# A hybrid attention and gating block in fp32: the order from the first norm to the sixth product written out on four engines

## The chip, the cores and the metric

The kernel runs on one core of a Trainium2 chip. Its work is shared by TensorE (PE, matrix products and transposes), VectorE (DVE), ScalarE (ACT), GpSimd (POOL) and the queues that issue DMA transfers, the main one on SyncE (SP). The metric is the device time of one execution in microseconds.

## The reference

One residual block over 1024 positions of width 1024: a norm, one wide projection `w_in`, a gated linear attention and a spatial gating unit, their merge, and a SwiGLU feed-forward layer, all in fp32.

```python
a = rmsnorm(x, norm_pre_mix[l])
proj = jnp.einsum('bsd,de->bse', a, w_in[l])
q, k, v, r, a_low, su, sv, g_gla, g_sgu = jnp.split(proj, IN_OFFSETS, axis=-1)
y_gla = gla_branch(q, k, v, r, a_low, w_gate_up[l], b_gate[l], gla_norm[l])
y_sgu = sgu_branch(su, sv, sgu_ln_g[l], sgu_ln_b[l], w_spatial[l], b_spatial[l])
merged = (jax.nn.sigmoid(g_gla) * jnp.einsum('bsv,vd->bsd', y_gla, w_branch_gla[l])
          + jax.nn.sigmoid(g_sgu) * jnp.einsum('bsv,vd->bsd', y_sgu, w_branch_sgu[l]))
x = x + rmsnorm(jnp.einsum('bsd,de->bse', merged, w_out[l]), norm_post_mix[l])
h = rmsnorm(x, norm_pre_ffn[l])
gate, up = jnp.split(jnp.einsum('bsd,df->bsf', h, w_ffn_in[l]), 2, axis=-1)
y = jnp.einsum('bsf,fd->bsd', jax.nn.silu(gate) * up, w_ffn_out[l])
x = x + rmsnorm(y, norm_post_ffn[l])
```

## The kernel before

An fp32 product is made of three products of rounded parts: each operand is split into hi (ScalarE's copy to the type fp32r, L86) and lo (VectorE's difference, L87), and `prod3` multiplies hi by hi, hi by lo and lo by hi (L110, L111, L112). The large products are blocked in two by two and need seven products of blocks instead of eight. In place of the eighth product stand sums and differences of blocks of both operands (`wsum` or, in place, `raw` for the weights), numbered m1 to m7; a product of one such number is 12 matmuls of 128x512.

A `Pair` is two blocks of 128 output columns, fetched as two raw weight tiles. `prepare(m)` makes the weight sum if m needs one (m5 and m7 at L257, m6 at L262, m4 at L265) and splits it; `product(m)` issues the 12 matmuls and then `collect`, which adds the results up on VectorE and ScalarE. m1 reads the first half of the columns of x tiles 4 to 7 and m2 the second half, m5 reads the sum of both halves of tiles 0 to 3. A `Stream` runs the pairs; its first three (the trio: su0, su1 and kq0 here) are taken together: m1 of su0 and su1, m2 of both, m1 and m2 of kq0, then m5 of the three, m7, m6, m4 and m3. There are two streams, over `w_in` from the start and over `w_ffn_in` from about 920 us.

At the start, the gain row is spread over 128 partitions by two matmuls (gb). Then for each of the tiles 4, 5, 6, 7, 0, 1, 2, 3 `norm_tile` squares the tile on ScalarE with the sum along the row, forms the factor on VectorE (L105) and GpSimd (a pow, L101), scales 1024 columns on VectorE (L406), and `A.tile` turns them by eight TensorE transposes into two PSUM banks (L170) and copies these to the raw tiles in SBUF on ScalarE (L172). From the raw tiles `first` splits for m1 and m2 (tiles 4 to 7), `second` adds the halves and splits for m5 (tiles 0 to 3), both at L86 and L87.

PSUM has eight banks, four of them for accumulators (`bank`), four for transposes and the like (`tbank`). The order on each engine is set by the scheduler of the tile framework, apart from SP's, which is written out; an engine works off its list in that order, and an instruction that waits holds up all behind it.

Of the kernel before, what the change touches and what calls it, by code (L numbers as in the profile page):

```python
# [10 lines left out]
AF = mybir.ActivationFunctionType  # L11
ALU = mybir.AluOpType
# [3 lines left out]
P = 128  # L16
D = 1024
# [14 lines left out]
def hybrid_block(ctx, tc, I, out):  # L32
    nc = tc.nc
# [34 lines left out]
    def slot(name, shape=(P, 1024), dt=F32):  # L68
        return px.tile(list(shape), dt, tag="X", name=name)
# [12 lines left out]
    def small(name, shape):  # L82
        return pm.tile(shape, F32, tag="m", name=name)
# [5 lines left out]
    def by4(t):  # L89
        return t.rearrange("p (a b) -> p a b", a=4)  # L90
# [6 lines left out]
    ident = cst.tile([P, P], F32, name="ident")  # L97
# [45 lines left out]
    class Operands:  # L143
# [11 lines left out]
                self.raw[r, c] = big(F32, f"{self.name}raw{r}{c}")  # L155
            return self.raw[r, c]

        def put(self, m, src, cols):
            if m not in self.hl:
                self.hl[m] = (big(F32R, f"{self.name}h{m}"), big(F32R, f"{self.name}l{m}"))  # L160
            hi, lo = self.hl[m]
            return split(hi[:, :, cols], lo[:, :, cols], src)

        def tile(self, row, tt, gains=None):
            r = 1 - tt // 4
            cols = slice((tt % 4) * P, (tt % 4) * P + P)
            for c in range(2):
                b = tbank(f"tp_{self.name}{tt}{c}")
                for j in range(4):
                    nc.tensor.transpose(b[:, j * P : (j + 1) * P], row[:, (c * 4 + j) * P : (c * 4 + j + 1) * P], ident)  # L170
                if gains is None:
                    nc.scalar.activation(self.quad(r, c)[:, :, cols], by4(b), AF.Copy)  # L172
                    continue
                for j in range(4):
                    nc.scalar.activation(self.quad(r, c)[:, j, cols], b[:, j * P : (j + 1) * P], AF.Copy,
                                         scale=gains[:, c * 4 + j : c * 4 + j + 1])

        def first(self, tt):
            cols = slice((tt % 4) * P, (tt % 4) * P + P)
# [40 lines left out]
    ORDER = (1, 7, 6, 5, 2, 4, 3)  # L220

    behind = {}

    class Pair:

# [24 lines left out]
        def prepare(self, m):  # L250

            a, b = self.raw
            w11, w12, w21, w22 = a[:, :, 0:P], a[:, :, P:256], b[:, :, 0:P], b[:, :, P:256]
            tt = nc.vector.tensor_tensor
            if m in (5, 7):
                src = w12 if self.trio and m == 7 else py.tile([P, 4, P], F32, tag="Y", name=f"wsum_{self.name}{m}")
                tt(out=src, in0=(w12, w22)[m == 7], in1=(w11, w12)[m == 7], op=ALU.subtract)  # L257
                if m == 7:
                    self.chain = src
            elif m == 6:  # L260
                src = self.chain
# [10 lines left out]
        def product(self, m, A):  # L272
            hi, lo = A.hl[m]
            w = self.w.pop(m)
            base = {2: 1, 4: 7, 3: None if self.p5 else 5}.get(m)
            new = tbank if self.trio and m == 6 else bank
            acc = self.acc[m] = self.acc[base] if base else new(f"{self.name}_m{m}")
            for k in range(4):
                prod3(acc, w[:, 0, k], w[:, 1, k], hi[:, k], lo[:, k], base is None and k == 0, k == 3, base is not None)
            self.collect(m, acc)  # L280

        def collect(self, m, acc):

# [44 lines left out]
    LEAD = 2  # L328

    class Stream:  # L330
# [69 lines left out]
    def norm_tile(tt):  # L400
        xt = xts[tt]
        a = slot(f"a_{tt}")
        ss = small(f"ss_{tt}", [P, 1])
        nc.scalar.activation(a, xt, AF.Square, accum_out=ss)
        rs = rsqrt_mean(ss, D, f"a{tt}")
        nc.vector.scalar_tensor_tensor(out=a, in0=xt, scalar=rs, in1=g_pre, op0=ALU.mult, op1=ALU.mult)  # L406
        A.tile(a, tt)
# [404 lines left out]
    one_row = slot("one_row", (1, P))  # L812
    nc.vector.memset(one_row, 1.0)
    g_pre = slot("g_pre")
    for j in range(2):
        b = tbank(f"gb_{j}")
        nc.tensor.matmul(b, lhsT=one_row, rhs=g_row[:, j * 512 : j * 512 + 512], start=True, stop=True)
        nc.vector.tensor_copy(g_pre[:, j * 512 : j * 512 + 512], b)
    for tt in (4, 5, 6, 7):
        norm_tile(tt)  # L820
        A.first(tt)
    stream.prepare(4)
    for tt in (0, 1, 2, 3):
# [247 lines left out]
    for half, j, fin in ((1, 0, False), (1, 1, True), (0, 1, False), (0, 0, True)):  # L1071
        w = wo10 if (half, j) == (1, 0) else out_weights(half, j)
        for tt in range(half * 4, half * 4 + 4):
            acc = (tbank if (half, j) == (1, 0) else bank)(f"wo_{tt}{j}")
            c = slice((tt % 4) * P, (tt % 4) * P + P)
            for kt in range(KT):
                hi, lo = mT[kt // 4][half]
# [7 lines left out]
            mix, ss = mixes[tt]  # L1085
            scaled_half(mix, ss, acc, j, g_pm)
            if fin:
                if tt in (2, 3):
                    xt = slot(f"xr_{tt}")
                    nc.sync.dma_start(out=xt, in_=x[tt * P : (tt + 1) * P, :])  # L1090
                else:
                    xt = load(f"xr_{tt}", x[tt * P : (tt + 1) * P, :])
                rs = both(ss, f"pm{tt}")
# [3 lines left out]
                rs = rsqrt_mean(ss[:, 3:4], D, f"pf{tt}")  # L1097
# [102 lines left out]
```

## Time and profile before

| | us |
|---|---|
| median of 3 runs | 1552.12 (1550.65 to 1552.93) |
| the profiled execution | 1552.86 |
| its span | 1550.9 |
| PE busy in it | 1523.6 (98%) |
| DVE, ACT, POOL busy | 1130.2, 661.6, 177.8 |

The span is the part of an execution that the profile covers. Busy time is the union of an engine's instructions, so that PE's idle time is the span less 1523.6 us. For matmuls the profile models the ends: a matmul starts each 0.23 us at full clock, and its row shows 0.39 us.

### The profile page before, as it was taken

To read this page: it belongs to the slowest core of one execution; us is meant where nothing else is said; L and a number is where in the kernel's file an instruction comes from. 1 tells how busy PE (TensorE), PEld (TensorE's weight loads), DVE (VectorE), ACT (ScalarE), POOL (GpSimd) and SP (SyncE) were. 2 spreads that over 40 slices of the span, in tenths; PEclk is the share of its full clock that TensorE was granted. 3 is DMA by queue.
4 is the path that set the end of the run, shared out by engine and by line. 5 is a ranking of instruction groups with operands and counts; after the bars stand their busy time and mean duration, and the time that the engine had idled before them with its cause. 6 is when DMAs were issued, how large, how long until landed. Compare 5 with 4: busy or idle time off the path is not lost.

```text
span 1550.9 us, 19786 instructions
## 1 busy us (share of the span) xinstructions
PE 1523.6 (98%) x7061; PEld 1243.9 (80%) x7061; DVE 1130.2 (73%) x1853; ACT 661.6 (43%) x1100; POOL 177.8 (11%) x275
## 2 busy tenths in 40 slices
PE   6999999899999999999999999999999999999998
PEld 5778777677888888888888887888888888888886
DVE  7966676577888878648796769877777876564547
ACT  7566333344444343444333675333333333363442
POOL 2112111011211111000000110111111110000002
PEclk9999999999999999999999999999999999999999
DMA  5134453245664364488972631656555643875653
GB/s 192 32 123 124 148 177 123 69 152 181 216 218 157 129 213 139 162 313 300 346 275 90 208 119 55 221 194 202 188 176 161 200 158 102 302 267 174 226 157 129
DMA packets 181844, 276.06 MB, mean 178 GB/s; under 512 B 10801, under 2 KB 108625, under 8 KB 181746
## 3 DMA queue, kind: packets, MB, share of 16 engines
q1 hardware_dynamic: 157714, 190.35, 38.5%
q0 software_dynamic: 24032, 84.45, 14.8%
q8 instruction: 56, 0.92, 0.2%
q14 instruction: 42, 0.34, 0.1%
HBM read 188.48 MB, written 86.28 MB: 177 GB/s over the span
## 4 chain that ended last, share of the span: by engine, by line
PE 94%; DVE 3%; ACT 1%; issue 1%; DMA 0%; POOL 0%; SPq 0%; DVEq 0%; POOLq 0%; ACTq 0%
PE f_m L110 8%; PE f_m L112 8%; PE f_m L111 8%; PE fo L110 5%; PE fo L111 5%; PE fo L112 5%; PE g_m L110 3%; PE g_m L112 3%; PE g_m L111 3%; PE wo L110 2%; PE wo L111 2%; PE wo L112 2%; PE kq_m L110 2%; PE su_m L111 2%; PE kq_m L112 2%; PE su_m L112 2%
## 5 line engine op out<-in xcount | busy, mean ns | idle before, releaser
L110 PE MATMUL f_m<-hh,w_f 128*128 128x512 f32 x616 | 239.7, 390 | 1.8 <-ACT w_f L86 1.1
L111 PE MATMUL f_m<-hl,w_f 128*128 128x512 f32 x616 | 239.8, 389 | 0.0
L112 PE MATMUL f_m<-hh,w_f 128*128 128x512 f32 x616 | 239.5, 389 | 0.0
L110 PEld LDWEIGHTS f_m<-hh,w_f 128*128 128x128 f32 x616 | 115.6, 188 | 26.3 <-issue 1.5
L112 PEld LDWEIGHTS f_m<-hh,w_f 128*128 128x128 f32 x616 | 115.6, 188 | 24.2 <-DVE w_f L87 0.2
L111 PEld LDWEIGHTS f_m<-hl,w_f 128*128 128x128 f32 x616 | 115.6, 188 | 24.1
L111 PE MATMUL fo<-fow,foa 128*128 128x512 f32 (+1 forms) x315 | 120.9, 384 | 0.0
L112 PE MATMUL fo<-fow,foa 128*128 128x512 f32 (+1 forms) x315 | 120.9, 384 | 0.0
L110 PE MATMUL fo<-fow,foa 128*128 128x512 f32 (+1 forms) x315 | 118.9, 385 | 0.5 <-DVE foc L935 0.5
L86 ACT ACTIVATE w_f<-raw_f 128x512 fp32r<-128x512 f32 x75 | 47.2, 633 | 104.7 <-PE f_m L112 88.5
L86 ACT ACTIVATE w_f<-wsum_f 128x512 fp32r<-128x512 f32 x79 | 49.9, 633 | 95.2 <-PE f_m L112 52.8
L87 DVE TENSOR_TENSOR w_f<-wsum_f,w_f 128x512 fp32r<-128x512 f32 x79 | 54.3, 688 | 48.1 <-ACT w_f L86 47.6
L111 PE MATMUL g_m<-al,w_g 128*128 128x512 f32 x224 | 88.3, 394 | 0.0
L110 PE MATMUL g_m<-ah,w_g 128*128 128x512 f32 x224 | 88.2, 394 | 0.0
L112 PE MATMUL g_m<-ah,w_g 128*128 128x512 f32 x224 | 87.8, 392 | 0.0
L87 DVE TENSOR_TENSOR foa<-fora,foa 128x1024 fp32r<-128x1024 f32 (+1 forms) x42 | 47.6, 1133 | 43.1 <-ACT foa L86 43.0
L86 ACT ACTIVATE foa<-fora 128x1024 fp32r<-128x1024 f32 (+1 forms) x42 | 41.5, 988 | 73.7 <-DMA fora<-fs_d 62.3
L110 PEld LDWEIGHTS fo<-fow,foa 128*128 128x128 f32 x315 | 59.2, 188 | 12.6 <-DVE foc L935 0.7
L112 PEld LDWEIGHTS fo<-fow,foa 128*128 128x128 f32 x315 | 59.2, 188 | 11.8
L111 PEld LDWEIGHTS fo<-fow,foa 128*128 128x128 f32 x315 | 59.2, 188 | 11.6
L87 DVE TENSOR_TENSOR fow<-forw,fow 128x1024 fp32r<-128x1024 f32 (+1 forms) x42 | 47.4, 1129 | 9.9 <-ACT fow L86 9.8
L87 DVE TENSOR_TENSOR w_f<-raw_f,w_f 128x512 fp32r<-128x512 f32 x75 | 51.2, 685 | 4.1 <-ACT w_f L86 3.9
(396 smaller groups left out, 3698.0 us busy)
## 6 DMA issues: line engine op xcount, KB each, us to landing
raw_f<-in_w_ffn_in SPq DMA_DIRECT2D x88, 256.0 KB, 3.4
fora<-fs_d SPq DMA_DIRECT2D x35, 512.0 KB, 4.4
fs_d<-f_o POOLq DMA_DIRECT2D x22, 512.0 KB, 3.8
w2e<-in_w_ffn_out SPq DMA_DIRECT2D x44, 256.0 KB, 4.5
ws_d<-w2e POOLq DMA_DIRECT2D x22, 512.0 KB, 3.7
forw<-ws_d SPq DMA_DIRECT2D x20, 512.0 KB, 4.7
raw_g<-in_w_in SPq DMA_DIRECT2D x16, 512.0 KB, 3.8
g_d<-g_o POOLq DMA_DIRECT2D x16, 512.0 KB, 4.8
```

Source lines behind the costliest of these rows:

```text
L86: a = nc.scalar.activation(hi, src, AF.Copy)
L87: return a, nc.vector.tensor_tensor(out=lo, in0=src, in1=hi, op=ALU.subtract)
L110: nc.tensor.matmul(acc, lhsT=lh, rhs=rh, start=first, stop=False, skip_group_check=onto)
L111: nc.tensor.matmul(acc, lhsT=lh, rhs=rl, start=False, stop=False, skip_group_check=onto)
L112: nc.tensor.matmul(acc, lhsT=ll, rhs=rh, start=False, stop=last, skip_group_check=onto)
```

## The change

`norm_tile` is gone. Its steps are now small functions, and the order of PE, ACT, DVE and POOL from the gain row through the sixth product is written out. hi of tiles 4 to 7 is copied straight from the transposes' PSUM bank (`high`), lo is the difference of the bank and hi (`low_part`), and the raw copies (`keep`) come later. The scale of tiles 4 to 7 is done in halves, and the bank for a tile's second half is an accumulator's for some. `fifth` adds the halves of tiles 0 to 3 from the bank of one and the raw copy of the other. `collect` of the first six products is put into the list `later_on` and called where the order says. The weights of the low-rank gate (`wa`) are fetched on GpSimd's queue before the pows. The weight sums of both trios are made by GpSimd (in the second stream all but m5's, by `early`).

```diff
-            tt = nc.vector.tensor_tensor
+            tt = (nc.gpsimd if self.trio and (m != 5 or early) else nc.vector).tensor_tensor
...
-            self.collect(m, acc)
+            if later_on is not None:
+                later_on.append(lambda: self.collect(m, acc))
+            else:
+                self.collect(m, acc)
...
-    for tt in (4, 5, 6, 7):
-        norm_tile(tt)
-        A.first(tt)
-    stream.prepare(4)
-    for tt in (0, 1, 2, 3):
-        norm_tile(tt)
-        A.second(tt)
+    def high(tt, c):
+        cols = slice((tt - 4) * P, (tt - 4) * P + P)
+        nc.scalar.activation(A.parts(1 + c)[0][:, :, cols], by4(turned[tt, c]), AF.Copy)
+
+    def low_part(tt, c):
+        cols = slice((tt - 4) * P, (tt - 4) * P + P)
+        hi, lo = A.parts(1 + c)
+        nc.vector.tensor_tensor(out=lo[:, :, cols], in0=by4(turned[tt, c]), in1=hi[:, :, cols], op=ALU.subtract)
+
+    def keep(tt, c):
+        A.keep(tt, c, turned[tt, c])
+
+    def fifth(tt):
+        cols = slice(tt * P, tt * P + P)
+        s1 = A.quad(2, 0)[:, :, cols]
+        nc.vector.tensor_tensor(out=s1, in0=by4(turned[tt, 1]), in1=A.raw[1, 0][:, :, cols], op=ALU.add)
+        A.put(5, s1, cols)
...
     low_rank_weights()
-    stream.fetch(3)
-    stream.run(6)
-    low_rank_sums()
+    with tc.manual_schedule(engines={ET.PE, ET.Activation, ET.DVE, ET.Pool}):
...
+        stream.prepare(1)
+        high(6, 0), low_part(6, 0), high(7, 0), low_part(7, 0)
+        go()
+        stream.prepare(2)
+        scale(6, 1), turn(6, 1, bank)
+        keep(4, 0)
+        high(4, 1), high(5, 1)
+        scale(7, 1), turn(7, 1, tbank)
+        low_part(4, 1), low_part(5, 1)
+        keep(4, 1)
+        high(6, 1), low_part(6, 1)
+        square(0)
+        high(7, 1), low_part(7, 1)
+        go()
...
+        for tt in (0, 1):
+            for c in range(2):
+                turn(tt, c, tbank)
+        scale(2, 0, 1)
+        keep(0, 0), keep(1, 0)
+        square(3), factor(3)
+        go()
+        stream.prepare(6)
+        fifth(0), fifth(1)
+        keep(0, 1), keep(1, 1)
+        scale(3, 0, 1)
+        for tt in (2, 3):
+            for c in range(2):
+                turn(tt, c, tbank)
+        keep(2, 0), keep(3, 0)
+        later_on[4]()
+        go()
+        fifth(2), fifth(3)
+        keep(2, 1), keep(3, 1)
+        keep(6, 1)
+        stream.prepare(7)
+        low_rank_sums()
+        for i in (2, 3, 5):
+            later_on[i]()
+    later_on = None
     stream.run(3)
...
+    early = False
```

`go` runs one product with the next weights not yet prepared; `turn` issues the four transposes of a half tile. The order moves on each engine as follows. First VectorE before, from the factor of tile 2 on: `a` is a scaled tile, `araw` a raw one or the sum of two, `al` lo of the activations, `w_kq` lo of the weights of kq.

```order
35 L105 TENSOR_SCALAR rs_a_322<-ss_320 128x1
36 L186 TENSOR_TENSOR araw_291<-araw_282,araw_289 128x4x128
37 L105 TENSOR_SCALAR rs_a_344<-ss_342 128x1
38 L406 SCALAR_TENSOR_TENSOR a_319<-xx_147,rs_a_322,g_pre 128x1024
39 L186 TENSOR_TENSOR araw_291<-araw_282,araw_289 128x4x128
40 L406 SCALAR_TENSOR_TENSOR a_341<-xx_147,rs_a_344,g_pre 128x1024
41 L87 TENSOR_TENSOR al_294<-araw_291,ah_293 128x4x128
42 L87 TENSOR_TENSOR w_kq_402<-raw_kq_366,w_kq_402 128x512
43 L87 TENSOR_TENSOR al_294<-araw_291,ah_293 128x4x128
```

The same place in the changed kernel, from the fifth product's weights on.

```order
36 L87 TENSOR_TENSOR w_kq_355<-raw_kq_349,w_kq_355 128x512
37 L837 SCALAR_TENSOR_TENSOR a_330<-xx_147,rs_a_334,g_pre 128x1024
38 L105 TENSOR_SCALAR rs_a_388<-ss_386 128x1
39 L87 TENSOR_TENSOR w_kq_404<-raw_kq_352,w_kq_404 128x512
40 L860 TENSOR_TENSOR araw_407<-tp_a_366,araw_382 128x4x128
41 L87 TENSOR_TENSOR al_410<-araw_407,ah_409 128x4x128
42 L860 TENSOR_TENSOR araw_407<-tp_a_376,araw_382 128x4x128
43 L87 TENSOR_TENSOR al_410<-araw_407,ah_409 128x4x128
44 L837 SCALAR_TENSOR_TENSOR a_385<-xx_147,rs_a_388,g_pre 128x1024
```

Before, the scales of tiles 2 and 3 (rows 38 and 40) stand two rows apart, and one sum of halves lies between them; now both `fifth` steps of tiles 0 and 1 (rows 40 to 43) stand between the scale of tile 2 (row 37) and that of tile 3 (row 44).

Then ScalarE before, after the first copy of a transposes' bank: L172 are the raw copies, L86 with `ah` hi of the activations.

```order
7 L86 ACTIVATE w_su_258<-raw_su_136 128x512
8 L172 ACTIVATE araw_179<-tp_a_174 128x4x128
9 L86 ACTIVATE ah_181<-araw_172 128x4x128
10 L172 ACTIVATE araw_172<-tp_a_196 128x4x128
11 L86 ACTIVATE ah_185<-araw_179 128x4x128
12 L172 ACTIVATE araw_179<-tp_a_202 128x4x128
13 L86 ACTIVATE ah_181<-araw_172 128x4x128
14 L404 ACTIVATE a_270,ss_271<-xx_140 128x1024
```

ScalarE in the changed kernel, from the first weight split on: L847 is hi from the bank, L187 a raw copy, L829 the square, `w_su_251` the weights of the second pair.

```order
8 L86 ACTIVATE w_su_231<-raw_su_136 128x512
9 L847 ACTIVATE ah_213<-tp_a_218 128x4x128
10 L847 ACTIVATE ah_213<-tp_a_225 128x4x128
11 L86 ACTIVATE w_su_251<-raw_su_143 128x512
12 L187 ACTIVATE araw_260<-tp_a_175 128x4x128
13 L847 ACTIVATE ah_262<-tp_a_187 128x4x128
14 L847 ACTIVATE ah_262<-tp_a_205 128x4x128
15 L187 ACTIVATE araw_274<-tp_a_187 128x4x128
16 L847 ACTIVATE ah_262<-tp_a_255 128x4x128
17 L829 ACTIVATE a_278,ss_279<-xx_140 128x1024
```

The raw copies have gone behind the first splits, and the weight split of the second pair (row 11) stands ahead of the first of them and of all splits for m2.

Last GpSimd in the changed kernel, from the last of the eight pows on; before, the memset of `aw` followed the pows there.

```order
24 L101 TENSOR_TENSOR rs_a_388<-rs_a_388,mhalf 128x1
25 L270 TENSOR_TENSOR wsum_su_465<-raw_su_136 128x512
26 L270 TENSOR_TENSOR wsum_su_510<-raw_su_143 128x512
27 L270 TENSOR_TENSOR raw_su_136<-raw_su_138,raw_su_136 128x4x128
28 L270 TENSOR_TENSOR raw_su_143<-raw_su_145,raw_su_143 128x4x128
29 L270 TENSOR_TENSOR wsum_kq_515<-raw_kq_349 128x512
30 L270 TENSOR_TENSOR raw_kq_349<-raw_kq_352,raw_kq_349 128x4x128
31 L275 TENSOR_TENSOR raw_su_136<-raw_su_136 128x4x128
32 L275 TENSOR_TENSOR raw_su_143<-raw_su_143 128x4x128
```

The weight sums (L270) follow the last pow (row 24) in the order m5 and m7 of su0 and su1, then those of kq0.

## Rows read from the trace of the kernel before

**Rows 1.** The page: busy time by engine, and the chain that ended last

```profile
PE 1523.6 (98%) x7061; PEld 1243.9 (80%) x7061; DVE 1130.2 (73%) x1853; ACT 661.6 (43%) x1100; POOL 177.8 (11%) x275
...
PE 94%; DVE 3%; ACT 1%; issue 1%; DMA 0%; POOL 0%; SPq 0%; DVEq 0%; POOLq 0%; ACTq 0%
```

**Rows 2.** Waits of PE: engine, line, releaser: us in total, times, longest

```profile
PE tp_a L170 <- ACT w_su L86: 4.9, 1, 4.9
PE tp_a L170 <- DVE a L406: 3.9, 2, 2.9
...
PE o L630 <- DVE st L621: 3.2, 1, 3.2
PE f_m L110 <- ACT w_f L86: 1.1, 1, 1.1
PE gg L549 <- ACT lh L86: 1.0, 1, 1.0
...
PE f_m L110 <- ACT f_u L302: 0.7, 1, 0.7
```

**Rows 3.** Windows: us, busy by engine (x), granted clock, DMA share, GB/s

```profile
10.00:20.00 10.00, 5.96 (x32) 5.09 (x32) 9.05 (x15) 9.81 (x21) 3.38 (x4) 1.00 1.06 381
...
60.00:80.00 20.00, 20.00 (x90) 16.57 (x89) 20.00 (x33) 7.49 (x11) 6.89 (x14) 1.00 0.24 65
...
940.00:960.00 20.00, 18.87 (x83) 15.14 (x82) 20.00 (x31) 8.73 (x14) 0.00 (x0) 1.00 0.19 54
```

**Rows 4.** PE in time: start, us, engine, line, operation [idle before, releaser]

```profile
21.81 1.82 PE L170 MATMUL tp_a<-ident,a 128*128 128x128 f32 x8 [4.93 <-ACT w_su L86]
...
27.07 0.78 PE L111 MATMUL su_m<-al,w_su 128*128 128x512 f32 x1
...
40.26 0.39 PE L110 MATMUL kq_m<-ah,w_kq 128*128 128x512 f32 x1
...
43.07 2.36 PE L473 MATMUL al<-araw,wa 128*32 128x256 f32 x40
...
49.75 0.50 PE L110 MATMUL su_m<-ah,w_su 128*128 128x512 f32 x1
```

**Rows 5.** ACT in order of time

```profile
10.46 1.06 ACT L404 ACTIVATE a<-xx 128x1024 f32<-128x1024 f32 x1 [0.19 <-DMA xx<-in_x]
...
11.51 0.58 ACT L172 ACTIVATE araw<-tp_a 128x512 f32<-128x512 f32 x1
11.99 0.62 ACT L86 ACTIVATE w_su<-raw_su 128x512 fp32r<-128x512 f32 x1
...
98.19 1.28 ACT L537 ACT_TABLE_LOAD   x1
```

**Rows 6.** DVE in order of time, 18 to 22 us

```profile
18.66 0.68 DVE L87 TENSOR_TENSOR al<-araw,ah 128x512 fp32r<-128x512 f32 x1
19.26 0.68 DVE L257 TENSOR_TENSOR wsum_su<-raw_su 128x512 f32<-128x512 f32 x1
20.38 1.28 DVE L406 SCALAR_TENSOR_TENSOR a<-xx,rs_a,g_pre 128x1024 f32<-128x1024 f32 x1 [0.44 <-POOL rs_a L101]
```

**Rows 7.** DMA issues from 0 to 40 us: size, median us to landing

```profile
raw_su<-in_w_in SPq DMA_DIRECT2D x4, 512.0 KB, 9.6
```

**Rows 8.** Windows with half the clock granted, columns as in rows 3

```profile
22.00:28.00 6.00, 5.01 (x20) 4.20 (x19) 6.00 (x12) 5.88 (x12) 2.33 (x4) 0.50 0.23 53
302.00:305.00 3.00, 3.00 (x16) 1.73 (x12) 0.17 (x1) 0.84 (x4) 0.28 (x1) 0.50 0.00 0
```

**Rows 9.** POOL in order of time

```profile
7.87 0.55 POOL L101 TENSOR_TENSOR rs_a<-rs_a,mhalf 128x1 f32<-128x1 f32 x1 [5.41 <-DVE rs_a L105]
...
18.82 1.53 POOL L101 TENSOR_TENSOR rs_a<-rs_a,mhalf 128x1 f32<-128x1 f32 x1 [5.15 <-DVE rs_a L105]
...
66.62 0.53 POOL L483 MEMSET aw<- 128x512 f32 x1 [37.28 <-DVE al L87]
```

**Rows 10.** ACT at the start of the feed-forward stage

```profile
952.80 0.63 ACT L86 ACTIVATE w_f<-raw_f 128x512 fp32r<-128x512 f32 x1 [4.04 <-DVE raw_f L265]
```

More of the change, by code (lines that the diff above doesn't have):

```diff
@@ L156, in quad, with parts, put @@
             return self.raw[r, c]
-        def put(self, m, src, cols):
+        def parts(self, m):
             if m not in self.hl:
                 self.hl[m] = (big(F32R, f"{self.name}h{m}"), big(F32R, f"{self.name}l{m}"))
-            hi, lo = self.hl[m]
+            return self.hl[m]
+        def put(self, m, src, cols):
+            hi, lo = self.parts(m)
             return split(hi[:, :, cols], lo[:, :, cols], src)
@@ L176, in tile, with turn, keep @@
                                          scale=gains[:, c * 4 + j : c * 4 + j + 1])
+        def turn(self, row, c, b):
+            for j in range(4):
+                nc.tensor.transpose(b[:, j * P : (j + 1) * P], row[:, (c * 4 + j) * P : (c * 4 + j + 1) * P], ident)
+        def keep(self, tt, c, b):
+            cols = slice((tt % 4) * P, (tt % 4) * P + P)
+            nc.scalar.activation(self.quad(1 - tt // 4, c)[:, :, cols], by4(b), AF.Copy)
         def first(self, tt):
@@ L222, in hybrid_block @@
     behind = {}
+    later_on = None
+    early = True
     class Pair:
@@ L272, in product @@
         def product(self, m, A):
+            nonlocal later_on
             hi, lo = A.hl[m]
@@ L365, in prepare, with run @@
                 self.ready += 1
-        def run(self, n=None, fill=0):
+        def run(self, n=None, fill=0, lead=LEAD):
             end = len(self.todo) if n is None else min(len(self.todo), self.at + n)
@@ L370, in run @@
                 p, m = self.todo[self.at]
-                self.prepare(self.at + 1 + LEAD)
+                self.prepare(self.at + 1 + lead)
                 if self.at >= self.hold:
@@ L399, in hybrid_block @@
     A = Operands("a")
[L400 to L407, printed above, removed]
     def store(dst, t):
@@ L814, in hybrid_block, with square, factor, scale @@
     g_pre = slot("g_pre")
-    for j in range(2):
+    ET = mybir.EngineType
+    later_on = []
+    norm, turned = {}, {}
+    def square(tt):
+        norm[tt] = (slot(f"a_{tt}"), small(f"ss_{tt}", [P, 1]))
+        nc.scalar.activation(norm[tt][0], xts[tt], AF.Square, accum_out=norm[tt][1])
+    def factor(tt):
+        norm[tt] += (rsqrt_mean(norm[tt][1], D, f"a{tt}"),)
+    def scale(tt, *cs):
+        a, _, rs = norm[tt]
+        cols = slice(cs[0] * 512, cs[-1] * 512 + 512)
+        nc.vector.scalar_tensor_tensor(out=a[:, cols], in0=xts[tt][:, cols], scalar=rs, in1=g_pre[:, cols],
+                                       op0=ALU.mult, op1=ALU.mult)
@@ new lines, in turn @@
+    def turn(tt, c, new):
+        b = turned[tt, c] = new(f"tp_a{tt}{c}")
+        for j in range(4):
+            nc.tensor.transpose(b[:, j * P : (j + 1) * P], norm[tt][0][:, (c * 4 + j) * P : (c * 4 + j + 1) * P], ident)
+    def high(tt, c):
[5 more added lines that the diff above has]
+        nc.vector.tensor_tensor(out=lo[:, :, cols], in0=by4(turned[tt, c]), in1=hi[:, :, cols], op=ALU.subtract)
@@ L816, in hybrid_block, with go, gb @@
+    def keep(tt, c):
[5 more added lines that the diff above has]
+        A.put(5, s1, cols)
+    def go():
+        stream.run(1, lead=0)
+    def gb(j):
         b = tbank(f"gb_{j}")
         nc.tensor.matmul(b, lhsT=one_row, rhs=g_row[:, j * 512 : j * 512 + 512], start=True, stop=True)
-        nc.vector.tensor_copy(g_pre[:, j * 512 : j * 512 + 512], b)
@@ L819, in hybrid_block @@
-    for tt in (4, 5, 6, 7):
-        norm_tile(tt)
-        A.first(tt)
-    stream.prepare(4)
-    for tt in (0, 1, 2, 3):
-        norm_tile(tt)
-        A.second(tt)
-    low_rank_weights()
-    stream.fetch(3)
-    stream.run(6)
-    low_rank_sums()
+        return nc.vector.tensor_copy(g_pre[:, j * 512 : j * 512 + 512], b)
+    low_rank_weights()
+    with tc.manual_schedule(engines={ET.PE, ET.Activation, ET.DVE, ET.Pool}):
+        gb(0)
+        square(4), square(5)
+        factor(4)
+        gb(1)
+        scale(4, 0), turn(4, 0, tbank)
+        square(6), factor(5)
+        scale(4, 1), turn(4, 1, bank)
+        scale(5, 0), turn(5, 0, tbank)
+        square(7), factor(6)
+        scale(5, 1), turn(5, 1, bank)
+        factor(7)
+        high(4, 0), high(5, 0)
+        scale(6, 0), turn(6, 0, tbank)
+        low_part(4, 0)
+        scale(7, 0), turn(7, 0, tbank)
+        low_part(5, 0)
+        stream.prepare(1)
[12 more added lines that the diff above has]
+        go()
+        later_on[0]()
+        stream.prepare(3)
+        square(1), factor(0)
+        go()
+        stream.prepare(4)
+        scale(0, 0, 1), factor(1)
+        later_on[1]()
+        keep(5, 0), keep(6, 0)
+        square(2)
+        scale(1, 0, 1), factor(2)
+        go()
+        stream.prepare(5)
+        keep(7, 0), keep(7, 1)
+        keep(5, 1)
+        for tt in (0, 1):
[4 more added lines that the diff above has]
+        square(3), factor(3)
+        go()
+        stream.prepare(6)
[7 more added lines that the diff above has]
+        later_on[4]()
+        go()
+        fifth(2), fifth(3)
[5 more added lines that the diff above has]
+            later_on[i]()
@@ L830, in hybrid_block @@
+    later_on = None
     stream.run(3)
```

## The prediction, made before the result was known

> **What bounds the kernel now.** I read the page first. TensorE is busy 98% of the span and the chain that ended last is 94% PE [rows 1], so only TensorE's idle time, 27.3 us of the span's 1550.9, is to be had or to be made worse. The list of waits says where it lies [rows 2]: 4.9 and 3.9 us while the first transposes wait for ScalarE and VectorE, 3.2 us around an output tile near 300 us, 1.1 us at the first weights of the feed-forward product, 1.0 us at the decay sums. The windows show what else is full there [rows 3]: from 10 to 20 us VectorE is busy 9.05 of 10 us and ScalarE 9.81, TensorE only 5.96. VectorE is again full from 60 to 80 us (20.00 of 20) and at the start of the feed-forward stage. Then TensorE's order of time [rows 4]: the first product gets its steady run at 27.07 us, the fifth product (kq, m1) starts at 40.26, and the seventh, the first that reads the sum of two row halves (m5), at 49.75. From 27 us on TensorE hardly waits. So the seventh product is the mark: what the change is worth at the start is how much earlier than 49.75 it begins, and whether TensorE keeps going after it.
>
> **The start: a lead of 10 us.** Prices: on ScalarE a 512-wide copy or split follows the one before by about 0.5 us, and a square takes 1.06 us, with about 0.2 for reading out its sum [rows 5]; on VectorE a 512-wide operation takes 0.68 and follows after 0.60, the 1024-wide scale 1.28 [rows 6]; a product is 40.26 to 43.07, 2.8 us, and eight transposes 1.82 at half the clock, so about 0.9 at the whole [rows 4, 8]. Before, all of x tiles 4 to 7 is scaled, turned, copied raw and split, and in between tiles 0 and 1 are squared and the second half's splits done, ahead of the first steady product. Now only half of each of the four tiles must be through: the square of tile 7 ends at about 11.7 [rows 5], then 0.15 for the factor, about 0.9 for a pow beside VectorE, a half scale 0.68, four transposes 0.9 at the slow clock of the start, hi 0.5 and lo 0.6, with a wait of about half a microsecond between VectorE's other operations: first product near 16.2 instead of 27.07.
>
> **How it thins.** ScalarE's new order puts the split of the second pair's weights ahead of the raw copies of tile 4. That pair's loads land a median 9.6 us after issue [rows 7]; its first reader on VectorE before was at 19.26 [rows 6]. I take 17.5 to 18, so ScalarE stands idle about 2 us and all that is queued behind it (copy, three splits, copy, square) is late; TensorE's next transposes need the bank that one of these copies frees. I go along each engine's written order with the prices above. ScalarE: weight split until 18.6, copy and three more until 20.6; transposes and handovers 1.1: second product 21.7. ScalarE again: split of tile 6, square of tile 0, split of tile 7, copy of the first accumulator, weight split, some 3.4 us to 24.0; low part 0.60: third product 24.7, fourth 27.6. Then sixteen transposes, 30.4 to 32.1, and the fifth product, 32.1 to 34.8. Before, five products and all transposes were done at 43.07; now the transposes of tiles 2 and 3 are still to come, about 1.8 us, so the same state could be reached at 36.6: a lead of 6.5 us is left.
>
> **The bubble that takes the rest.** The last eight transposes, those of tile 3, wait for its scale. In VectorE's order this stands behind the two `fifth` steps of tiles 0 and 1, and each is a bounce: add 0.60 on VectorE, split on ScalarE 0.5 and a handover, low part 0.60 on VectorE. They begin when the raw copies, the square of tile 3 and the sixth weight split are done on ScalarE, about 34.3, and end about 38.3; the scale, 1.20, ends near 39.9. TensorE, through with tile 2 at 35.7, waits 4.2 us, and then 0.9 more, since the sixth product's bank goes through the collecting copy of kq, queued behind a raw copy. 6.5 - 5.1 is 1.4 us ahead of before.
>
> **GpSimd's sums.** Twelve weight sums of 0.60 leave VectorE, 7.2 us. No row shows a two-input sum of 128x512 on GpSimd; below stands the 0.53 of a memset of the same tile [rows 9], above three times that, 1.6, a pass for each operand; I take 1.1, the middle. They start after the last pow, about 34.7, and even at 1.6 the sixth is there at 44.3, in time for its product. Their length then costs nothing. Their company may: a pow on one element, usually 0.55, took 1.53 us while VectorE ran two sums from SBUF [rows 9, 6], so VectorE can hold GpSimd up. The other way round, VectorE held by a sum, no row shows. Two low parts of the bounce fall beside these sums; held for one sum each, 2 x 1.1, they make the bubble 6.3 us, and the seventh product comes 0.7 us later than before. Between -1.4 and +0.7 I take 0.0, nearer the held case, since a hold in one direction is in the trace. [...]
>
> **The clock.** After 4.93 us without work TensorE ran at 0.50 of its clock from 22 to 28 us, and after 3.2 us near 301 us again [rows 2, 4, 8]: 6.8 and 3.4 us at half speed, so 3.4 and 1.7 us of loss. A bubble of 4 to 6 us is of that size and now stands in front of dense products. The slow stretch of before lies over the first transposes and matmuls, and its cost is in the 27.07 already counted. Bounds 0 and +3.4; I take +2.5.
>
> **Further on.** The small transposes and the decay logits stand earlier in TensorE's order. The 1.0 us at the decay sums [rows 2] should go; but a product's bank is now freed by an add that VectorE has queued behind the logits' steps, which wait for ScalarE's exp and log with two table loads of 1.28 [rows 5]. Bounds -1.0 and +2.6; I take +1.0, near the middle. VectorE has no slack from 60 to 80 us [rows 3], so what is late at the seventh product is not made up. The early wa load has its consumer at 43 us and moves 64 KB, 0.2 us at the 381 GB/s of rows 3, by which the loads behind it come later. At the feed-forward start nine sums move to GpSimd: TensorE waits only 1.1 + 0.7 us there [rows 2], which bounds the gain at 1.8; VectorE is full [rows 3] and ScalarE waits 4.04 us for one of these sums [rows 10]; nine sums holding VectorE 1.1 instead of occupying it 0.60 would be 4.5 us of delay, of which some 3 could reach TensorE. Between -1.8 and +3 I take 0.
>
> **Sum.** 0.0 + 2.5 + 1.0 + 0 = +3.5. The profiled execution took 1552.86 us (span 1550.9), 0.74 above the median of 1552.12; so 1556.4 for it, and 1555.6 as a median. The lowest sum of the bounds is -1.4 + 0 - 1.0 - 1.8 = -4.2, the highest 0.7 + 3.4 + 2.6 + 3 = +9.7.
>
> **Rivals.** (a) The lead stays. If ScalarE's and VectorE's bounce is shorter than I walk it (the adds beginning 2 us sooner, the second pair landing at 17), the bubble is under 2 us, the clock doesn't fall, and 4.5 us of the 6.5 are kept, on a VectorE relieved of 7.2 us: 1547.6. For it: of the 27 us of idle time most lies before 27 us, so there is something to win. Against: VectorE and ScalarE are full in that stretch and their work before the seventh product shrinks only by the sums. (b) No change: bubble and lead cancel, the clock falls only shortly, the decay wait goes: -0.7 + 1.0 + 0, about 1552.4. For it: PE is fed from the same VectorE work either way. (c) Held VectorE everywhere: GpSimd's sums hold it in the bounce (+0.7), again in the feed-forward start (+3), with the full clock loss (+3.4) and the late bank (+1): +8.1, 1560.2.
>
> **Chances.** A measurement of this kernel tells about 0.2%, 3.1 us, from no change. Forecast (bubble and half clock, +2.5 to +6) 0.36, of which 0.05 lies below +3.1; (b) 0.28; (a) 0.26; (c) 0.10. So faster 0.26, same 0.33, slower 0.41. For 8 in 10 the range leaves a tenth below and above: 1546.5 to 1560; the forecast's own is 1554.6 to 1558.1.
>
> **What would show it.** In the changed kernel's profile: the first product at 16 to 17 us; ScalarE idle about 2 us at 15 to 18 with the second pair's weights as its release; the fifth product at 31 to 33; TensorE idle 4 to 6 us just ahead of the last eight transposes of tiles 2 and 3, released by VectorE's scale; a granted clock of 0.5 after it; the seventh product at 48 to 51. VectorE low parts longer than 0.68 beside GpSimd's sums would show the hold. A seventh product before 46, or no bubble, refutes the forecast and leaves (a); low parts at 0.68 beside a running sum refute (c).

## The result: 20 us slower, in three stretches

The changed kernel takes 1573.0 us in the median (1572.61 to 1573.84), the kernel before 1552.53 in the same comparison: ratio 1.0135, 95% interval 1.012 to 1.015. The forecast was 1555.6 with a range from 1546.5 to 1560; the sign was right, the size not. The measured +20.5 is twice the highest sum of the prediction's bounds (+9.7).

The page of the changed kernel, the two lines that answer to [rows 1]:

```profile
PE 1531.3 (97%) x7061; PEld 1247.3 (79%) x7061; DVE 1138.0 (72%) x1836; ACT 663.1 (42%) x1101; POOL 219.4 (14%) x296
...
PE 89%; DVE 5%; DMA 2%; issue 1%; ACT 1%; POOL 0%; SPq 0%; POOLq 0%; DVEq 0%; ACTq 0%
```

TensorE issues the same 7061 matmuls. Its idle time has gone from 27.3 us to 1571.0 - 1531.3 = 39.7, and its busy time is 7.7 us longer, at the same work and at a mean granted clock of 0.991 instead of 0.996: nearly all of it is time at the lower clock, by an estimate from the two clocks and spans (0.009 x 1571.0 - 0.004 x 1550.9 = 7.9 us). GpSimd's 41.6 us more are the 21 weight sums. VectorE, which has lost these 21 sums, is busy 7.8 us longer with fewer instructions. The waits of PE, to be held against [rows 2] (engine, line, releaser: us in total, times, longest):

```profile
PE tp_a L843 <- DVE a L837: 6.4, 2, 6.0
PE f_m L110 <- DVE f_u L325: 5.3, 2, 3.3
PE lg L525 <- DVE vecs L502: 4.6, 1, 4.6
...
PE f_m L110 <- ACT f_u L319: 2.6, 1, 2.6
PE tp_a L843 <- DVE rs_a L105: 2.1, 1, 2.1
PE kq_m L112 <- DVE w_kq L87: 1.0, 1, 1.0
```

The 4.9 us of before are gone. In their place stand a wait of 6.0 us for a scaled tile, one of 4.6 for the small vectors behind the decay logits, and 8 us at the feed-forward start, where there were 1.8.

To see where the time goes, the start of each hi-by-hi matmul (L110) in the other kernel's trace less that of the same one (the n-th of its name) before, in us; the column on the left is its start before. The first three lines do not compare equal work. At 36.81 the kernel before has all 64 transposes behind it and the others 32, which is some 4 us of the lead shown; at 23.29 it is 40 and 24. And of the small products `al` (3.9 us), 2.4 us stood ahead of the matmul at 45.36 before and stand behind it in all others, so at that line 2.4 us have to be added. At 49.75, the seventh product, and at 55.34 the work done is the same in all.

| start before | change | e1 | e8 | e12 |
|---|---|---|---|---|
| 23.29 | -7.6 | -6.8 | -6.5 | -7.4 |
| 36.81 | -9.3 | -8.6 | -8.7 | -8.5 |
| 45.36 | -0.7 | -1.7 | -6.2 | -4.9 |
| 49.75 | +3.0 | +2.3 | -4.0 | -1.2 |
| 55.34 | +3.0 | +2.9 | +1.1 | -1.2 |
| 70.52 | +3.8 | +4.1 | +1.3 | -1.0 |
| 83.22 | +12.0 | +5.4 | +1.1 | -1.2 |
| 120.86 | +11.4 | +7.4 | +1.4 | -0.9 |
| 905.05 | +11.3 | +6.8 | +2.0 | -0.3 |
| 999.53 | +20.2 | +6.9 | +2.1 | -0.3 |

The lead is there, some 5.5 us of it at equal work, and it is gone at 45 us (-0.7 + 2.4 = +1.7). Then some 10 us are lost until 83 us, most of them behind 70 us, and 9 more between 925 and 975 us. PE in order of time, answering to [rows 4] (start, us, engine, line, operation, idle before and releaser):

```profile
15.74 0.49 PE L110 MATMUL su_m<-ah,w_su 128*128 128x512 f32 x1 [0.69 <-ACT ah L847]
...
42.44 1.94 PE L843 MATMUL tp_a<-ident,a 128*128 128x128 f32 x8 [6.00 <-DVE a L837]
44.70 0.79 PE L110 MATMUL kq_m<-ah,w_kq 128*128 128x512 f32 x1 [0.32 <-ACT kq_u L319]
49.11 3.66 PE L481 MATMUL al<-araw,wa 128*32 128x256 f32 x64
```

The first product starts at 15.74 (before, its steady run began at 27.07). The last eight transposes wait 6.00 us, and the seventh product comes when `al` ends, at 52.70. The windows (columns as in [rows 3]):

```profile
40.00:50.00 10.00, 7.24 (x37) 5.35 (x41) 6.97 (x8) 5.99 (x11) 0.55 (x1) 0.66 0.00 2
...
60.00:80.00 20.00, 18.13 (x78) 14.01 (x76) 20.00 (x21) 7.40 (x12) 12.60 (x14) 1.00 0.06 13
80.00:100.00 20.00, 15.23 (x67) 11.93 (x68) 11.31 (x20) 11.97 (x22) 6.55 (x11) 0.83 0.50 155
...
960.00:980.00 20.00, 14.23 (x59) 10.51 (x58) 18.64 (x24) 4.12 (x8) 5.03 (x3) 0.99 0.20 55
```

Two readings matter. The granted clock is 0.66 on average in the ten microseconds that hold the end of the 6 us of idle time and what follows, and 0.83 in the twenty around the 4.6 us at the logits. And from 60 to 80 us VectorE is full with 21 instructions, where before it was full with 33 [rows 3]: each has become longer.

### The profile page after: what moved, and what is told of

Same layout as the page of the kernel before. It is cut to its first block, busy times and chain, and to the rows that moved or that the text cites. A ratio compares the mean times of both kernels' runs of the same rounds, so it can differ in the third digit from the quotient of the medians.

```text
span 1571.0 us, 19824 instructions
## 1 busy us (share of the span) xinstructions
PE 1531.3 (97%) x7061; PEld 1247.3 (79%) x7061; DVE 1138.0 (72%) x1836; ACT 663.1 (42%) x1101; POOL 219.4 (14%) x296
## 4 chain that ended last, share of the span: by engine, by line
PE 89%; DVE 5%; DMA 2%; issue 1%; ACT 1%; POOL 0%; SPq 0%; POOLq 0%; DVEq 0%; ACTq 0%
PE f_m L110 8%; PE f_m L111 8%; PE f_m L112 8%; PE fo L110 4%; PE fo L111 4%; PE fo L112 4%; PE g_m L110 3%; PE g_m L112 3%; PE g_m L111 3%; PE wo L110 2%; PE wo L112 2%; PE wo L111 2%; PE v_m L110 2%; PE r_m L110 2%; PE sv_m L110 2%; PE r_m L112 2%
## 5 line engine op out<-in xcount | busy, mean ns | idle before, releaser
L110 PE MATMUL f_m<-hh,w_f 128*128 128x512 f32 x616 | 240.7, 391 | 8.0 <-DVE f_u L325 5.3
L110 PEld LDWEIGHTS f_m<-hh,w_f 128*128 128x128 f32 x616 | 116.1, 188 | 33.7 <-issue 6.6
L110 PE MATMUL fo<-fow,foa 128*128 128x512 f32 (+1 forms) x315 | 118.9, 385 | 0.5 <-DVE foc L1048 0.5
L86 ACT ACTIVATE w_f<-raw_f 128x512 fp32r<-128x512 f32 x75 | 47.2, 633 | 107.6 <-PE f_m L112 97.5
L86 ACT ACTIVATE w_f<-wsum_f 128x512 fp32r<-128x512 f32 x79 | 50.0, 633 | 91.5 <-PE f_m L112 55.0
L110 PE MATMUL g_m<-ah,w_g 128*128 128x512 f32 x224 | 88.2, 394 | 0.0
L86 ACT ACTIVATE foa<-fora 128x1024 fp32r<-128x1024 f32 (+1 forms) x42 | 41.5, 987 | 74.9 <-DMA fora<-fs_d 63.3
L110 PEld LDWEIGHTS fo<-fow,foa 128*128 128x128 f32 x315 | 59.2, 188 | 12.4 <-DVE foc L1048 0.7
```

The source lines that it names most:

```text
L86: a = nc.scalar.activation(hi, src, AF.Copy)
L110: nc.tensor.matmul(acc, lhsT=lh, rhs=rh, start=first, stop=False, skip_group_check=onto)
```

## What GpSimd's sums do to VectorE

VectorE of the changed kernel at the bounce, in order of time:

```profile
35.21 0.68 DVE L860 TENSOR_TENSOR araw<-tp_a,araw 128x512 f32<-128x512 f32 x1
36.59 1.62 DVE L87 TENSOR_TENSOR al<-araw,ah 128x512 fp32r<-128x512 f32 x1 [0.70 <-ACT ah L86]
38.13 0.68 DVE L860 TENSOR_TENSOR araw<-tp_a,araw 128x512 f32<-128x512 f32 x1
39.50 1.60 DVE L87 TENSOR_TENSOR al<-araw,ah 128x512 fp32r<-128x512 f32 x1 [0.69 <-ACT ah L86]
```

and GpSimd beside it, with the fifth, sixth and last of the twelve sums:

```profile
34.89 2.76 POOL L270 TENSOR_TENSOR wsum_su<-raw_su 128x512 f32<-128x512 f32 x2
37.62 2.93 POOL L270 TENSOR_TENSOR raw_su<-raw_su,raw_su 128x512 f32<-128x512 f32 x2
50.96 2.20 POOL L270 TENSOR_TENSOR wsum_kq<-raw_kq 128x512 f32<-128x512 f32 x1 [10.40 <-DVE w_su L87]
53.24 1.63 POOL L270 TENSOR_TENSOR raw_kq<-raw_kq,raw_kq 128x512 f32<-128x512 f32 x1
...
82.23 1.29 POOL L278 TENSOR_TENSOR raw_kq<-raw_kq,raw_kq 128x512 f32<-128x512 f32 x1
```

The add from PSUM (L860, one operand in SBUF) keeps its 0.68 us beside a running sum. The low part with both operands in SBUF takes 1.62 instead of the 0.68 of [rows 6]: it is held for 0.94 us. The hold works the other way round too, and worse. GpSimd and ScalarE in the feed-forward stage:

```profile
948.52 7.95 POOL L275 TENSOR_TENSOR raw_f<-raw_f 128x512 f32<-128x512 f32 x1 [5.77 <-DVE w_f L87]
```

```profile
956.50 0.63 ACT L86 ACTIVATE w_f<-raw_f 128x512 fp32r<-128x512 f32 x1 [2.12 <-POOL raw_f L275]
```

This one sum takes 7.95 us, while four at the bounce take 5.7. VectorE runs operations with two SBUF operands back to back from 948.36 to 955.32 us, and GpSimd doesn't come in between: the sum ends at 956.46, 1.14 us behind that run. ScalarE waits for the sum, and the low part, VectorE's next work, for ScalarE. So a sum on GpSimd cost VectorE about a microsecond where it was already running (0.94 us at 36.59), and came late beside a run of VectorE's (7.95 us at 948.52).

## The experiments

Theories: (1) GpSimd's sums hold VectorE and are late, and that is nearly all of the loss; (2) the written-out order itself loses at the start. Twelve kernels were run. In the diffs `...` marks lines left out.

**e1 and e2: the sums back on VectorE.** e1 in both streams, e2 in the second alone.

```diff
-            tt = (nc.gpsimd if self.trio and (m != 5 or early) else nc.vector).tensor_tensor
+            tt = nc.vector.tensor_tensor                                            # e1
+            tt = (nc.gpsimd if self.trio and early else nc.vector).tensor_tensor    # e2
```

> The changed kernel with all weight sums of the trios back on VectorE; the written-out order stays. In the changed kernel TensorE is 11.3 us late at 120 us and loses 8.9 us more between 925 and 975 us. Theory 1 (GpSimd's sums hold VectorE's two-input operations and are late themselves, and that is nearly all of the loss): the feed-forward part goes to 0, the start to what the order alone costs, +1 to +4, so 1553.5 to 1557. Theory 2 (the written-out order itself loses the time at the start): only the 8.9 us of the feed-forward start come back, 1563 to 1565. VectorE's 128x512 low parts should be back at 0.68 us from 1.6.

> The changed kernel with the nine feed-forward weight sums back on VectorE, the first stage as changed. Theory 1 and theory 2 both give the start's 11.3 us and nothing more: 1563 to 1565. A rival for the feed-forward part (it is late because the start is late, or because instructions before it changed places, not because of its sums) gives 1571 to 1573.

Measured: e1 1560.0 (ratio 1.0051, 1.0036 to 1.0066), e2 1564.3 (1.0079, 1.0062 to 1.0096), against 1553.0 before. e2 is as forecast: the nine sums of the second stream cost 1573.0 - 1564.3 = 8.7 us (matmul by matmul, e2 is 11.5 us late at 1000 us where the changed kernel is 20.2, the same difference), and nothing of the start carries over to that stage. e1 lies between the theories: the sums of the start cost 1564.3 - 1560.0 = 4.3 us, the order itself 7.0. Both theories are needed; neither holds alone. The low parts of the feed-forward activations, grouped from 928 to 972 us (count, busy us, mean ns), in the changed kernel

```profile
L87 DVE TENSOR_TENSOR hl<-hraw,hh 128x512 fp32r<-128x512 f32 x7 | 7.8, 1151 | 0.1
```

and in e2

```profile
L87 DVE TENSOR_TENSOR hl<-hraw,hh 128x512 fp32r<-128x512 f32 x7 | 4.6, 687 | 0.1
```

**e3: the sums alone, on the kernel before.**

```diff
-            tt = nc.vector.tensor_tensor
+            tt = (nc.gpsimd if self.trio and (m != 5 or early) else nc.vector).tensor_tensor
```

> The kernel before with the trio's weight sums on GpSimd as in the change (all in the first stream, all but m5 in the second), no written-out order. Theory 1: the feed-forward start loses 7 to 10 us as in the changed kernel, the first stage another 3 to 9: 1562 to 1571. Theory 2: the first stage loses nothing from the sums, so 1559.5 to 1562.5.

Measured 1567.1, ratio 1.0097 (1.0082 to 1.0112): theory 1's range. The sums alone cost 14.1 us on the order of before and 13.0 on the written one (1573.0 - 1560.0), so the two causes add up within about a microsecond. The waits of PE:

```profile
PE tp_a L170 <- ACT w_su L86: 5.8, 1, 5.8
PE tp_a L170 <- DVE a L407: 5.0, 3, 3.4
PE f_m L110 <- DVE f_u L309: 4.5, 2, 2.4
PE lg L518 <- DVE vecs L495: 3.7, 1, 3.7
```

Matmul by matmul it is 3.3 us late at 45 us (here the sums stand between the norm's pows on GpSimd), 6.4 at 924 us and 15.3 at the end. The wait at `vecs` is there without the written-out order, and e1 hasn't got it; so it comes with the sums. The order of the scheduler moved with them in all three kernels, and what part of those 4 us is that and what part the hold was not separated.

**e4, e5 and e13: is it the read, the writing, or the late result?** The kernel before, with work on GpSimd that nobody reads: e4 six additions of 128x64 behind each of nine weight splits, e5 memsets instead, e13 twelve additions that read the low part just made.

```diff
+            if beside and self.trio and m in (7, 6, 4):
+                with tc.issue_after(low_w.ins):
+                    for _ in range(6):
+                        nc.gpsimd.tensor_tensor(out=spare, in0=ident[:, 0:64], in1=ident[:, 64:128], op=ALU.add)    # e4
+                        nc.gpsimd.memset(spare, 0.0)                                                                # e5
+                for i in range(12):                                                                                 # e13
+                    nc.gpsimd.tensor_tensor(out=spare, in0=w[:, 1, i % 4, 0:64].bitcast(F32), in1=ident[:, 0:64], op=ALU.add)
```

> The kernel before, all sums on VectorE, and on GpSimd, behind each of nine low parts of the feed-forward trio's weights, six additions of 128x64 from SBUF whose result nobody reads. Theory 1 (GpSimd operations that read SBUF hold VectorE's operations with two SBUF inputs): VectorE's 128x512 low parts there go from 0.68 to 0.9 us or more where they meet, and TensorE loses 2 to 6 us: 1555 to 1559. Rival (the sums cost because their results come late, not because the engines exclude each other): low parts stay at 0.68 us, 1552 to 1553.5.

> As the run with idle additions, with memsets of 128x64 in their place, which only write. Theory 1 with the read as what counts: low parts at 0.68 us, 1552 to 1553.5. If any GpSimd work beside VectorE holds it: the same loss as with the additions. Rival: 1552 to 1553.5.

> The kernel before with all sums on VectorE; behind each of the nine low parts of the feed-forward trio's weights (m7, m6, m4) GpSimd adds twelve times 128x64, reading that low part, into a tile nobody reads. The additions with idle operands ran at 391 to 423 us instead of here, behind other GpSimd work that VectorE needed; here nothing waits for GpSimd. Theory 1 (VectorE is held, by the reads alone, without any late sum): VectorE's 128x512 low parts that meet an addition go from 0.68 to about 0.8 us, and TensorE, which waits 1.1 us there, waits 2 to 6 us: 1554 to 1558. Rival (the 8.6 us of the feed-forward sums come from results that are late, not from the hold): 1552 to 1553.5.

Measured: e4 1557.5 (1.0028, 1.0018 to 1.0037), e5 1553.4 (1.0001, 0.9992 to 1.0011), e13 1578.3 (1.016, 1.0146 to 1.0174). e5 is as forecast, e4 falls into theory 1's range, though not for its reason, and e13 is outside both of its ranges. e4 and e5 missed their place: with no operand to wait for, the operations ran from 391 us on, not at the feed-forward start. They still tell the read from the write. VectorE in e4, beside additions,

```profile
394.92 0.81 DVE L87 TENSOR_TENSOR w_g<-wsum_g,w_g 128x512 fp32r<-128x512 f32 x1
395.66 0.54 DVE L695 TENSOR_TENSOR wbge<-wbge 128x256 f32<-128x256 f32 x1
```

and the same two in e5, beside memsets:

```profile
395.01 0.68 DVE L87 TENSOR_TENSOR w_g<-wsum_g,w_g 128x512 fp32r<-128x512 f32 x1
395.61 0.42 DVE L695 TENSOR_TENSOR wbge<-wbge 128x256 f32<-128x256 f32 x1
```

0.12 to 0.13 us more beside an addition of 64 columns, nothing beside a memset; 0.94 beside a sum of 512 columns is about eight times as much. So in these rows VectorE was held beside GpSimd instructions that read and not beside those that only write, and longer beside the one that read eight times the columns. Little of e4's 4.4 us is hold, since pows that VectorE waits for stood in GpSimd's queue behind the additions; these waits of VectorE in e4 (390 to 440 us) are not in the kernel before:

```profile
DVE vn L757 <- POOL rsv L101: 4.8, 2, 4.2
```

e13 was to settle what part of the feed-forward loss is hold, and didn't. GpSimd there, and what ScalarE waited for (us, times, longest):

```profile
934.49 13.53 POOL L274 TENSOR_TENSOR decay<-w_f,ident 128x64 f32<-128x64 f32 x1 [16.38 <-DVE w_f L87]
```

```profile
ACT w_f L86 <- POOL decay L274: 35.2, 7, 7.9
```

This time GpSimd was the one held. The first addition took 13.53 us, until VectorE's run of back-to-back operations was over at 947.84; the 54 additions of that size in e4 took 0.31 to 0.79 us, 0.32 in the median. VectorE's low parts mostly stayed at 0.69 and were not at the 0.8 expected. And the weights' buffers, which I had overlooked, stay taken until the additions have read them, so that ScalarE waited 35 us. It shows how dear a late GpSimd is where others wait for it; how the 8.7 us divide between hold and lateness stays open.

**e6 and e8: the bubble.** On e1, e6 moves only the scale of tile 3 ahead; e8 moves also the sums of halves and the raw copies that free the banks.

```diff
-        fifth(0), fifth(1)
-        keep(0, 1), keep(1, 1)
         scale(3, 0, 1)
+        fifth(0), fifth(1)                  # e6
+        keep(0, 1), keep(1, 1)
...
         keep(0, 0), keep(1, 0)
+        fifth(0, 1)                         # e8; step 1: the sum, step 2: its split
         square(3), factor(3)
+        fifth(1, 1)
+        keep(0, 1), keep(1, 1)
+        scale(3, 0, 1)
         go()
         stream.prepare(6)
-        fifth(0), fifth(1)
-        keep(0, 1), keep(1, 1)
-        scale(3, 0, 1)
+        fifth(0, 2), fifth(1, 2)
```

> As e1, and VectorE scales tile 3 before the two sums of halves of tiles 0 and 1 instead of after them. Theory B (the idle time ahead of the last eight transposes, 6.0 us in the changed kernel, is the wait for this scale): the idle time falls under 1.5 us, and the kernel is 3 to 5 us faster than e1, with the clock not falling there. Rival (the splits for the seventh product are as late as before and TensorE waits there instead): within 1 us of e1.

> The changed kernel with its sums on VectorE; the two sums of halves of tiles 0 and 1, their raw copies and the scale of tile 3 go ahead of the split for the sixth product and of both splits of these sums, so that neither the scale nor a bank is late for the last eight transposes. Theory B (the bubble of 4.2 us and the half clock behind it, about 2 us, are what the written order costs): idle time there under 1.5 us, no half clock, 4 to 6 us faster than 1560.0: 1554 to 1556. Theory V: VectorE stays full from 50 to 90 us, and at most 1.5 us are won: 1558.5 to 1560.

Measured: e6 1560.1, as e1 (1.0051 for both); e8 1554.6, ratio 1.0009 (1.0000 to 1.0019). Before the last eight transposes e1 waits

```profile
41.35 1.94 PE L843 MATMUL tp_a<-ident,a 128*128 128x128 f32 x8 [4.17 <-DVE a L837]
```

and e6 3.8 us, for another reason:

```profile
PE tp_a L843 <- ACT araw L187: 3.8, 1, 3.8
```

The banks for these transposes are those of tiles 0 and 1, free only when sum and raw copy have read them, and both stand behind the bounce. In e8 the transposes run through, and what is left is

```profile
39.19 0.50 PE L110 MATMUL kq_m<-ah,w_kq 128*128 128x512 f32 x1 [1.07 <-ACT kq_u L319]
```

with the clock at 1.00 from 40 to 50 us where e1 has 0.66. The sixth product starts 4.4 us earlier than in e1 (39.19 for 43.61) and the seventh 6.4 us: 3.1 us less idle time ahead of the sixth (4.17 - 1.07), and transposes and sixth product at full clock (e1's sixth product takes 4.9 us, 43.61 to 48.50, where one before took 2.8 [rows 4]). Then e8 loses 5.1 us until 55.34 (-4.0 to +1.1). TensorE waits 0.99 and 2.09 us for the weights of the seventh and eighth product, and with these waits the clock falls after all:

```profile
50.30 0.80 PE L112 MATMUL su_m<-ah,w_su 128*128 128x512 f32 x1 [2.09 <-DVE w_su L87]
```

The windows of e1 and of e8 (columns as in [rows 3]):

```profile
40.00:50.00 10.00, 8.33 (x48) 6.11 (x52) 7.00 (x10) 6.88 (x13) 0.00 (x0) 0.66 0.01 2
```

```profile
40.00:50.00 10.00, 7.21 (x78) 4.07 (x76) 9.30 (x12) 8.64 (x13) 0.00 (x0) 1.00 0.00 1
50.00:60.00 10.00, 9.71 (x36) 7.93 (x37) 10.00 (x14) 6.65 (x12) 0.00 (x0) 0.83 0.01 2
```

At 55.34 e8 is only 1.8 us ahead of e1; the rest of its gain comes behind that, where e1 loses 2.5 us more until 83 us and 2.0 until 121, e8 none and 0.3. e8 moved VectorE's work too (9.30 us of the ten busy, against 7.00 in e1), so its 5.4 us are not the bubble alone. Theory B was right in the time and for the wait ahead of the transposes, but its "no half clock" held only up to 50 us. e6's rival was right in the time alone: the wait stayed ahead of the transposes, for the banks, and did not move to the seventh product.

**e7, e10, e11 and e12: VectorE's late work.** e7 is e1 with four weight sums written into places where VectorE stood idle; e10 is e8 with them; e11 adds that the second pair's weights are split behind the raw copies; e12 adds that the weights of the seventh and eighth product are split earlier.

```diff
+        for m in (5, 7):
+            stream.order[0].prepare(m, 1)     # e7, e10 to e12: the sum alone; the same for su1
-        stream.prepare(2)                     # e11, e12: to here from the line after the first product
         keep(4, 1)
+        stream.prepare(2)
...
         fifth(0, 2), fifth(1, 2)
+        stream.prepare(8)                     # e12
...
-        stream.prepare(7)                     # e12
```

> The changed kernel with its sums on VectorE, and four of them (m5 and m7 of su0 and su1) written into the places where VectorE stood idle, near 17 and 24 us. Theory V (TensorE waits between 50 and 85 us because VectorE is full there, with work that the written order pushed behind it): 4 x 0.6 us leave that stretch, 1.5 to 2.5 us faster than the 1560.0 without it: 1557.5 to 1558.5. Rival (the bubble and the slow clock before 50 us are all that the order costs): 1559.5 to 1560.5, or slower since the start is held up.

> The closed bubble (1554.6 alone) and the four early sums (1.6 faster than without them) together. Theory V (what is left is work that VectorE does late: TensorE waits 2.1 and 1.0 us for the weights of the seventh and eighth product, which stand behind four sums on VectorE): those waits fall under 1 us and 1.5 to 2.5 us are won: 1552 to 1553. Rival (the two edits win the same time): 1554 to 1555.

> As the run before, and the split of the second pair's weights behind the raw copies and the first two splits for m2, so that ScalarE doesn't stand idle at 16 to 18 us for that pair's load. Theory: the second product starts 1.5 to 2.5 us earlier, and what of it reaches the seventh product is bounded by VectorE: 0 to 1.5 us faster than without it, 1551 to 1553. Rival (the low part of that split now comes late instead): no gain or up to 1 us slower.

> As the run before, and the weights of the seventh and eighth product are split ahead of the last two sums of halves instead of behind them. Theory V: the seventh product no longer waits for its weights, 1 to 2 us faster than without it: 1549.5 to 1552, under the kernel before. Rival (VectorE's total work until 90 us is the bound, and what moves ahead pushes back the splits for m7): within 0.7 us of the run before.

Measured: e7 1558.4 (1.0037), e10 1554.9 (1.0017, 1.0008 to 1.0026), e11 1553.7 (1.0011, 1.0002 to 1.0020), e12 1552.0 (0.9996, 0.9988 to 1.0005). e7 won 1.6 us, as theory V has it. In e10 the two gains don't add in the time, as its rival has it: matmul by matmul it is 0.8 us ahead of the kernel before at 102 us, where e8 is 1.0 behind, and 1.2 behind at 121 us; there TensorE waits 1.1 and 0.8 us at the decay sums, for ScalarE's and VectorE's splits. e11 and e12 won 1.2 and 1.7 us on the step before, as their theories have it, though e11 ends above the range given for it. The intervals of neighbours overlap, e7's and e1's too, so that no single step of 1 to 2 us is sure; the 2.9 us from e10 to e12 are. e12, the best, keeps 0.9 us of lead at 121 us and 0.3 to the end: no difference from the kernel before that can be measured. Its windows:

```profile
40.00:60.00 20.00, 19.57 (x126) 14.78 (x127) 19.80 (x25) 17.40 (x28) 0.00 (x0) 0.91 0.00 1
60.00:80.00 20.00, 20.00 (x90) 16.54 (x90) 19.85 (x33) 6.89 (x12) 7.43 (x14) 1.00 0.31 87
```

VectorE is full in both, as in [rows 3]. With 7 us of lead for the first product it still comes out even: part of that lead is transposes put off, 2.1 us go in a wait for the sixth product's bank with the lower clock behind it (0.91 on average from 40 to 60 us), and 1.2 us are left at the seventh product.

## Why the prediction was wrong

- **The lead, and its thinning:** right. The first product starts at 15.74 for 16.2; ScalarE waits 2.38 us for the second pair; the fifth product starts at 32.6 for 32.1.
- **The bubble:** right in place, cause and size, 6.00 us for the held 6.3, and 4.17 for the free 4.2 once the sums are gone (e1). "Held for one sum each, 2 x 1.1" was 0.94 and 0.92. (With 2.2 added to 4.2 the held bubble would have been 6.4 and the seventh product 0.8 late, not 6.3 and 0.7.) The 0.9 us for the sixth product's bank were 0.32.
- **The clock:** right at the bubble, where the window from 40 to 50 us has 0.66. A second fall, behind the 4.6 us at the logits (0.83 from 80 to 100 us), was not in the sum.
- **GpSimd's sums:** here the prediction failed, at "their length then costs nothing". I priced the hold at two low parts, of all the VectorE work that stands beside the twelve sums, and stopped at the seventh product. The sixth sum was not there at 44.3 us but at 54.9: the later sums wait for VectorE's splits of the tiles that they overwrite (10.40 us for the fifth), so the twelve stretch to 83.5 us, 1.25 to 2.3 us each instead of 1.1, alongside a VectorE that I had myself found full from 60 to 80 us. The term was 0.7 us at its highest; measured with e1 and e2 it is 4.3.
- **The feed-forward start:** I wrote that nine sums holding VectorE would be "4.5 us of delay, of which some 3 could reach TensorE" and took 0. It is 8.7 us (e2). The rows show both hold and lateness there, and I had put a price on the first alone; and where VectorE was shown full, the middle between a gain and a loss was no sound choice.
- **Further on:** +1.0 was taken for the order of the logits; the wait came (4.6 us at `vecs`, and the lower clock behind it), but with the sums, not with the order: e1 hasn't got it. What the order does cost there without them is the 2 us that e1 loses between 83 and 121 us.
- **The order's own price:** by the free case the sum would have been -1.4 + 2.5 + 1.0 = +2.1 us; e1 measures 7.0. Its seventh product starts at 52.09 (as `al`, 3.66 us, ends) for 49.75, 2.3 us late where bubble and clock gave 1.1. Then 3.1 us go until 83 us, in waits for weights' splits (the longest, 0.78 us, at 79.65) while VectorE is full with the sums and splits that the written order pushed behind it; I had named this ("what is late at the seventh product is not made up") and given it no price. Four sums moved out of that stretch gave 1.6 us back in the median (e7). The last 2.0 go between 83 and 121 us.

So the ledger: order 7.0, sums at the start 4.3, sums in the feed-forward stage 8.7, together 20.0. Rival (c) had the mechanism of 13.0 of these, at a chance of 0.10 and at less than a third of the price (0.7 and 3 us).

## What to carry to other kernels

The sums that left a full VectorE for GpSimd here did not leave it: beside one sum a VectorE operation of 512 columns with both operands in SBUF took 1.62 us instead of 0.68, while one with an operand in PSUM kept its 0.68. Look at which operands are in PSUM, and price every operation that such work meets, not only the one on the path. Where an order is written out, ask of each wait what else is queued for the same bank: e6 took one cause of the bubble away and met the second at once. An early start is worth only what the fullest engine can follow; move that engine's idle time forward before moving TensorE's.

## What the runs showed of the hardware

- A VectorE operation of 512 columns with two SBUF operands was held for 0.94 us by a GpSimd sum of 512 columns (1.62 us for 0.68, the changed kernel), one of 512 or 256 columns for 0.12 to 0.13 by an addition of 64 (0.81 and 0.54 us, e4, for 0.68 and 0.42, e5); with one operand in PSUM beside a sum (0.68 us), or beside memsets (0.68 and 0.42), VectorE was not held.
- The other way round, GpSimd was held while VectorE ran operations with two SBUF operands back to back: one sum of 512 columns took 7.95 us where two took 2.76 (the changed kernel), and one addition of 64 columns 13.53 us (e13) where the median in e4 was 0.32. They ended 1.14 and 0.18 us behind VectorE's runs, of 7 and 17 instructions.
- After 6.00 us (the changed kernel) and 4.17 us (e1) without work the granted clock was 0.66 on average in the window from 40 to 50 us. After 1.07 us (e8) it stayed at 1.00 there, and after two further waits of 0.99 and 2.09 us it was 0.83 from 50 to 60 us; in e12, after 2.11 us ahead of the sixth product, it was 0.91 from 40 to 60 us.
